# One transformer block on one core: dilated attention reads gathered operands, and the feed-forward part's last features and first tiles change order

## The chip, the cores and the metric

One NeuronCore of a Trainium2 chip runs the whole kernel, one launch. The metric is the device time of that launch in microseconds. Engines are named as in the profile: PE is TensorE (PEld its weight loads), DVE VectorE, ACT ScalarE, POOL GpSimd, SP SyncE, whose queue issues all the DMAs here.

## What is computed

The reference is one layer on x of 2048 tokens by 1024: an RMS norm, one input projection, four mixers side by side (dilated window attention, an RG-LRU, a Mamba-2 SSD, differential attention), an output projection, a norm and a residual, then a feed-forward part with a squared ReLU. Two parts matter here:

```python
DILATED_PATTERNS = ((128, 1), (512, 4), (2048, 16))
...
qb = strided(q)                      # [heads, dil, blocks, 128, 64]: every dil-th token
kc = with_prev(strided(k))           # a block of keys and the one before it
sc = jnp.einsum('bhrnqd,bhrnkd->bhrnqk', qb, kc).astype(jnp.float32) * scale + bias
...
f = jnp.square(jax.nn.relu(jnp.einsum('bsd,df->bsf', u, w_ff_up[layer])))
```

f then goes through w_ff_down, a norm and a residual. All inputs and outputs are f32. The kernel splits f32 operands into f16 high and low parts and adds up to three products of them.

## The kernel before, in words

**Order of work.** No engine's order is written out by hand. The kernel is recorded as many threads in named lanes (Loom, L305); weave (L442) then lists the instructions in the order in which it thinks they can start, and this static order is each engine's program. cost_of (L390) prices an instruction: an f16 matmul by its columns at 2390 a microsecond, whatever its stride; an ACT activation of n elements at 0.065 + n/1195 us; a POOL copy at 0.1 + 2.15 n/1000 us. A lane's priority shifts its planned start by 0.1 us a step (L469); a lower number goes first. All engines, SP included, work off their queues in order, so an instruction that waits holds up what stands behind it.

**Dilated attention** (L1072 to L1233) works on two pairs of heads, g = 0 and 1. dilated_pair loads f16 q, and f16 high and low keys (kh, kl), token by token along the free dimension, in two loads: the first 512 tokens, then the rest. Passes run in the order p = 1, 2, 0, with dil 4, 16 and 1, of 16 blocks each. For a block, dilated_block takes 128 queries as stationary operand, q[hh][:, qv], and 256 keys (128 for a first block) as moving operand, kh[hh][:, kv] and kl[:, hh, kv], where qv and kv are slices with step dil. Per head it adds a high and a low product, so four score matmuls "as" a block. Then DVE adds the bias and takes the extreme, ACT takes the exponential, PE transposes, DVE copies to SBUF, PE multiplies with v ("ao"), and DVE writes the result to its place in num. In pass 1 the blocks with n = 0, which need the first 512 tokens only, come first. After each pass its statistics go through DRAM; pass 0 ends with dilated_merge, whose sums run on POOL. Projections of the other mixers (tiles pt and pv) run in lanes of their own and stand between the blocks on PE.

**Feed-forward part** (class Ffn, L1622 to L1948). It is a seven-product scheme (Strassen's, Winograd's form) on halves of the operands. There are 16 pairs of feature tiles, g = 0 to 15, in PASSES (L37) of 2, 2, 3, 3, 3 and 3 pairs, and two token halves, cp. run (L1919) calls up_weights and up_block for each pair and half, in order of g; the last two blocks are (15, 1) and (15, 0). An up_block has 84 matmuls (lane up, priority 2), puts raw features e into DRAM (put, L1732; not for the pass that is used last), and up_operands (L1773, lane fform, priority 1) forms four sums on POOL (fz), splits seven operands on ACT and DVE (fs) and stores them (fO): for two of the four token tiles j with two stores, or for all four j with four stores in the pass that comes last in QS (L35), pass 5. The down products take the passes in the order QS = 1, 2, 0, 3, 4, 5, and within a pass cp = 0, 1 and j = 0, 1, 2, 3 (L1947). down_weights loads raw rows (dr), takes differences on POOL (ds) and splits them (dw). f_operands (L1814) loads the formed operands of a tile with an even j (fo from fO), and forms those of an odd j from raw features (fr, ft on POOL, then ACT and DVE). down_block (L1835) accumulates in the f32 tiles y. These lie in pool fd:

```python
k.fd = k.pool("fd", after=("fuw", "dk2"))     # L2036: opens when both are done with
```

fuw and dk2 hold the features, the temporaries and the splits of the up part, so y is first written after the last fs. Tiles 1 and up claim their y tiles before their first matmul in the plan.

Of the kernel before, what the change touches and what calls it, by code (L numbers as in the profile page):

```python
# [11 lines left out]
F16 = mybir.dt.float16  # L12
# [7 lines left out]
P = 128  # L20
S = 2048
# [1050 lines left out]
def dilated_attention(k, ap):  # L1072

    nc = k.nc
    bp = k.pool("apm", side="right", on=("w", "u", "stage"), after=("lru",))
    with nc.lane("aload"):
        q = [ap.tile([P, S], F16, tag=f"q{hh}", name=f"aq{hh}") for hh in range(2)]
        kh = [ap.tile([P, S], F16, tag=f"k{hh}", name=f"ak{hh}") for hh in range(2)]
        kl = ap.tile([P, 2, S], F16, tag="kl", name="akl")
    for g in range(2):  # L1080
        dilated_pair(k, ap, bp, g, q, kh, kl)


def token_view(a, dil):
# [5 lines left out]
    return [(slice(r * nb, (r + 1) * nb), v[r]) for r in range(dil)]  # L1090


def dilated_pair(k, ap, bp, g, q, kh, kl):
    nc = k.nc
    ms = ap.tile([P, 2, 2 * NT], F32, tag="ms", name=f"ams{g}")
    ds = ap.tile([P, 2, 2 * NT], F32, tag="ds", name=f"ads{g}")
    num = {}
    with nc.lane("aload"):
        f = score_scale(k, ap, 2 + g)
    for p in (1, 2, 0):  # L1100
        dil = DILS[p]
        nb = NT // dil
        va = k.vA[:, g * P:(g + 1) * P]
        with nc.lane("aload"):
            bias = ap.tile([P, 2, 256], F32, tag="bias", name=f"ab{g}{p}", bufs=2)
            for hh in range(2):
                toeplitz(k, bias[:, hh, :], skewed(k, g * 2 + hh, ND + p * NA, 256), 256, 0, 256)
            nc.gpsimd.tensor_scalar(bias[:], bias[:], f[:, 1:2], 1.0, op0=ALU.mult, op1=ALU.mult)
            v = ap.tile([P, NT, P], F32, tag="v", name=f"av{g}{p}", bufs=2)
            mt = ap.tile([P, NT, 2], F32, tag="mt", name=f"mt{g}{p}", bufs=2)  # L1110
            dt = ap.tile([P, NT, 2], F32, tag="dt", name=f"dt{g}{p}", bufs=2)
            if p:
                nm = num[p] = (ap if p == 1 else bp).tile([P, S], F32, tag=f"num{p}", name=f"num{g}{p}")
            if p == 1:
                for c0, c1 in ((0, 512), (512, S)):
                    sl = slice(c0, c1)
                    for hh in range(2):
                        rows, n = slice(hh * 64, hh * 64 + 64), c1 - c0
                        src = k.qA[g][rows, :, sl]
                        nc.sync.dma_start(q[hh][:, sl], src[0:1, 0:1, 0:1].custom([[S, P], [1, n]], [P, n], src))  # L1120
                        for x, t in ((0, kh[hh][:, sl]), (1, kl[:, hh, sl])):
                            src = k.kA[g][rows, x:x + 1, sl]
                            nc.sync.dma_start(t, src[0:1, 0:1, 0:1].custom([[2 * S, 64], [0, 2], [1, n]], [P, n], src))
                    for ch in range(c0 // 512, c1 // 512):
                        nc.sync.dma_start(v[:, ch:NT:4, :],
                                          va[ch * 512:ch * 512 + 512, :].rearrange("(i r) c -> i r c", r=4))
            elif p == 2:
                nc.sync.dma_start(v[:], va.rearrange("(i r) c -> i r c", r=16))
            else:
                nc.sync.dma_start(v[:], va.rearrange("(n i) c -> i n c", i=P))  # L1130
            if (g, p) == (0, 1):
                k.strips.append(skewed(k, 6, 0, S))
        if p:
            for n in range(nb):
                for r in range(dil):
                    with nc.lane("dil"):
                        dilated_block(k, ap, q, (kh, kl), v, bias, f, mt, dt, nm, 0, dil, r, n, r * nb + n)
            with nc.lane("astat"):
                for src, dst, nme in ((mt, ms, "m"), (dt, ds, "d")):
                    dram = k.dram.tile([S, 2], F32, tag=f"st{nme}{p}", name=f"ast{nme}{g}{p}")  # L1140
                    for sl, a in token_view(dram, dil):
                        nc.sync.dma_start(a, src[:, sl, :])
                    nc.sync.dma_start(dst[:, p - 1, :].rearrange("p (n h) -> p n h", h=2),
                                      dram.rearrange("(n i) h -> i n h", i=P))
            continue
        for ch in range(4):
            with nc.lane("dil"):
                nm = bp.tile([P, 512], F32, tag="num0", name=f"num{g}0{ch}", bufs=2)
                nc.claim(nm)
            for n in range(4 * ch, 4 * ch + 4):  # L1150
                with nc.lane("dil"):
                    dilated_block(k, ap, q, (kh, kl), v, bias, f, mt, dt, nm, ch * 512, 1, 0, n, n)
            with nc.lane("merge"):
                dilated_merge(k, bp, g, ch, nm, num, mt, dt, ms, ds)

# [39 lines left out]
    nc.sync.dma_start(k.mixT[ch][g * P:(g + 1) * P, :], nm[:])  # L1195


def dilated_block(k, ap, q, kt, v, bias, f, mt, dt, num, t0, dil, r, n, b):
    nc = k.nc
    lo = 0 if n else P  # L1200
    qv = slice(n * P * dil + r, n * P * dil + r + (P - 1) * dil + 1, dil)
    k0 = (n * P - (P - lo)) * dil + r
    kv = slice(k0, k0 + (255 - lo) * dil + 1, dil)
    es = []
    ps = k.psum.tile([P, 2, 256], F32, tag="S", name="as", bufs=2)
    with nc.fuse():
        for hh in range(2):
            nc.tensor.matmul(ps[:, hh, lo:256], q[hh][:, qv], kt[0][hh][:, kv], start=True, stop=False)
            nc.tensor.matmul(ps[:, hh, lo:256], q[hh][:, qv], kt[1][:, hh, kv], start=False, stop=True)
    for hh in range(2):  # L1210
        e = ap.tile([P, 256], F32, tag=f"e{hh}", name="ae", bufs=3)
        nc.vector.tensor_tensor_reduce(e[:, lo:256], ps[:, hh, lo:256], bias[:, hh, lo:256], f[:, 0:1], BIG, ALU.add, ALU.min,
                                       mt[:, b, hh:hh + 1])
        nc.scalar.activation(e[:, lo:256], e[:, lo:256], AF.Exp, bias=mt[:, b, hh:hh + 1], scale=-1.0,
                             accum_out=dt[:, b, hh:hh + 1])
        es.append(e)
    tp = turn(k, [P, 2, 256], b, "atp")
    with nc.fuse():
        for hh in range(2):
            for c in range(lo // P, 2):  # L1220
                nc.tensor.transpose(tp[:, hh, c * P:(c + 1) * P], es[hh][:, c * P:(c + 1) * P], k.ident)
    at = ap.tile([P, 2, 256], F32, tag="at", name="aat", bufs=2)
    if ATD(b):
        nc.vector.tensor_copy(at[:, :, lo:256], tp[:, :, lo:256])
    else:
        nc.scalar.activation(at[:, :, lo:256], tp[:, :, lo:256], AF.Copy)
    o = k.psum.tile([P, 512], F32, tag="O", name="ao", bufs=1)
    with nc.fuse():
        for c in range(lo // P, 2):
            for hh in range(2):  # L1230
                nc.tensor.matmul(o[hh * 64:(hh + 1) * 64, 0:P], v[:, b - 1 + c, hh * 64:(hh + 1) * 64],
                                 at[:, hh, c * P:(c + 1) * P], start=(c == lo // P), stop=(c == 1))
    nc.vector.tensor_copy(num[:, qv.start - t0:qv.stop - t0:dil], o[:, 0:P])  # L1233
# [388 lines left out]
class Ffn:  # L1622
# [87 lines left out]
    def up_block(self, g, cp):  # L1710
# [25 lines left out]
                nc.sync.dma_start(self.f[q, cp][j, :, x, :].rearrange("j p c -> p j c"),  # L1736
                                  e[f][:, j].rearrange("p j a t -> p j (a t)"))
        q = next(i for i, (p0, p1) in enumerate(PASSES) if p0 <= g < p1)
        with nc.lane("up", 2):
            X, Y, Z, V = self.banks(False)  # L1740
            nc.need(*u[TURN[-1]])
            s = k.fuw.tile([P, 512], F32, tag="s", name=f"us{g}{cp}", bufs=1)
# [25 lines left out]
            put(0)  # L1768
        self.made_last = e
        if q + cp:  # L1770
            self.up_operands(q, g - PASSES[q][0], cp, e)

    def up_operands(self, q, x, cp, e):  # L1773

        k, nc = self.k, self.k.nc
        with nc.lane("fform", 1, DVE=1.0):
            js = slice(0, 4, 1 if q == QS[-1] else 2)
            nj, ni = (4, 2) if q == QS[-1] else (2, 4)
            if e is None:
# [139 lines left out]
    def run(self):  # L1919
# [2 lines left out]
        self.fst = k.pool("fst", side="right", on=("ub",))  # L1922
        blocks = [(0, 0), (1, 0), (0, 1), (1, 1)] + [(g, cp) for g in range(2, n - 1) for cp in range(2)]
        blocks += [(n - 1, 1), (n - 1, 0)]
        ready = 0
        for g, cp in blocks:
            while ready < min(n, g + 2):
                self.up_weights(ready, 0 if ready < 3 else 1)
                ready += 1
                for x in range(8) if ready == 2 else (ready + 5,) if 2 < ready < 11 else ():  # L1930
                    self.down_top(x)
            self.up_block(g, cp)
            if self.made in (9, 13):
                self.up_operands(0, (self.made - 9) // 4, 0, None)
        self.down_scale()
# [2 lines left out]
        for n, q in enumerate(QS):  # L1938
# [5 lines left out]
                    self.gp = k.wpool.tile([P, D], F32, tag="wraw", name="fgp", bufs=2)  # L1944
                    nc.sync.dma_start(self.gp[:], self.post.to_broadcast([P, D]))
            for cp in range(2):
                for j in range(4):  # L1947
                    self.down_block(q, cp, j)  # L1948


# [131 lines left out]
```

## Time and profile before

| | before |
|---|---|
| median of three runs | 2567.38 us (2563.37 to 2567.38) |
| the profiled execution | 2568.09 us |
| its span, first to last instruction | 2566.3 us |
| mean granted TensorE clock | 0.985 |
| PE, DVE, ACT, POOL busy | 95%, 73%, 50%, 44% of the span |

The profiled execution lies 0.71 us above the median. Almost every instruction carries line 562 (L562), the place where the planner issues, so instructions are told apart by tile names: "as<-ak,aq" is a score matmul that reads the keys' tile ak and the queries' tile aq. Where a row starts with a time, that is the start in us from the span's start, followed by the duration. A matmul's duration includes the pipeline behind it; what one costs PE is the distance between two starts.

### The profile page before, as it was taken

To read this page: it belongs to the slowest core of one execution; us is meant where nothing else is said; L and a number is where in the kernel's file an instruction comes from. 1 tells how busy PE (TensorE), PEld (TensorE's weight loads), DVE (VectorE), ACT (ScalarE), POOL (GpSimd) and SP (SyncE) were. 2 spreads that over 40 slices of the span, in tenths; PEclk is the share of its full clock that TensorE was granted. 3 is DMA by queue.
4 is the path that set the end of the run, shared out by engine and by line. 5 is a ranking of instruction groups with operands and counts; after the bars stand their busy time and mean duration, and the time that the engine had idled before them with its cause. 6 is when DMAs were issued, how large, how long until landed. Compare 5 with 4: busy or idle time off the path is not lost.

```text
span 2566.3 us, 39805 instructions
## 1 busy us (share of the span) xinstructions
PE 2426.2 (95%) x14186; PEld 1285.8 (50%) x14186; DVE 1879.7 (73%) x3985; ACT 1280.9 (50%) x2677; POOL 1120.2 (44%) x1139
## 2 busy tenths in 40 slices
PE   7999999999999998999999999999997999999997
PEld 5555574765744455665445444444443444444443
DVE  6487887776689877867876776666657869868566
ACT  6367765443346667755535555555654413213221
POOL 5274331011155634455541444444435546645356
PEclk9999999999999998999999999999998999999999
DMA  6523215355251345235563444433325423323266
GB/s 190 152 67 93 87 60 166 91 137 125 61 151 60 104 128 150 93 92 164 173 222 108 143 156 142 153 106 109 115 102 184 145 76 109 123 86 124 81 202 194
DMA packets 286262, 322.28 MB, mean 126 GB/s; under 512 B 51508, under 2 KB 237300, under 8 KB 282991
## 3 DMA queue, kind: packets, MB, share of 16 engines
q1 hardware_dynamic: 286063, 319.74, 39.7%
q8 instruction: 112, 1.84, 0.3%
q14 instruction: 87, 0.71, 0.1%
HBM read 219.46 MB, written 107.03 MB: 127 GB/s over the span
## 4 chain that ended last, share of the span: by engine, by line
PE 59%; DVE 18%; DMA 8%; issue 5%; POOL 5%; ACT 3%; SPq 2%; DVEq 0%; POOLq 0%; ACTq 0%
PE mv L562 10%; PE mz L562 10%; PE mx L562 10%; PE my L562 5%; PE pt L562 4%; DVE e L562 4%; PE po L562 2%; DVE y L562 2%; PE as L562 2%; PE pv L562 2%; PE do L562 2%; SPq L562 2%; PE dt L562 2%; PE ao L562 1%; PE atp L562 1%
## 5 line engine op out<-in xcount | busy, mean ns | idle before, releaser
L562 PEld LDWEIGHTS <-fo 128*128 128x128 f16 x2688 | 263.4, 98 | 357.8 <-issue 37.7
L562 PEld LDWEIGHTS <-uw 128*128 128x128 f16 x2688 | 263.7, 98 | 314.4 <-issue 5.2
L562 PE MATMUL pt<-uuh,wl 128*128 128x512 f16 x640 | 243.3, 380 | 1.2 <-DVE wl L562 1.2
L562 PE MATMUL pt<-uuh,wh 128*128 128x512 f16 x640 | 243.6, 381 | 0.5 <-ACT dtraw L562 0.5
L562 PE MATMUL pt<-uul,wh 128*128 128x512 f16 x640 | 243.2, 380 | 0.0
L562 DVE CUSTOM_DVE_ANT_0 e<-sc,strip,scf 128x512 f32<-128x512 f32 (+3 forms) x320 | 205.9, 662 | 24.0 <-PE sc L562 14.4
L562 PE MATMUL mx<-dw,fo 128*128 128x512 f16 x768 | 183.6, 382 | 16.5 <-ACT ds L562 9.8
L562 PE MATMUL mz<-dw,fo 128*128 128x512 f16 x768 | 181.7, 379 | 13.1 <-DVE y L562 13.1
L562 ACT ACTIVATE e<-e,dmn 128x1024 f32<-128x1024 f32 (+4 forms) x192 | 171.4, 894 | 45.3 <-DVE dmn L562 42.6
L562 PEld LDWEIGHTS <-wh 128*128 128x128 f16 x1280 | 122.9, 98 | 126.0 <-issue 21.5
L562 PE MATMUL mv<-dw,fo 128*128 128x512 f16 x768 | 181.4, 379 | 1.9 <-DVE y L562 1.9
L562 POOL TENSOR_TENSOR y<-y,ds 128x512 f32<-128x512 f32 x72 | 112.9, 1584 | 153.7 <-DVE ds L562 153.7
L562 PE MATMUL mx<-u,uw 128*128 128x512 f16 x768 | 177.8, 381 | 2.0 <-DVE c L562 2.0
L562 PE MATMUL mv<-u,uw 128*128 128x512 f16 x768 | 178.3, 381 | 0.0
L562 PE MATMUL mz<-u,uw 128*128 128x512 f16 x768 | 176.5, 379 | 0.2 <-DVE c L562 0.2
L562 PE MATMUL po<-woh,mx 128*128 128x512 f16 x512 | 168.4, 384 | 0.0
L562 POOL TENSOR_SCALAR e<-e,dcf 128x256 f32<-128x256 f32 (+4 forms) x96 | 75.8, 790 | 166.5 <-DVE dcf L562 119.1
L562 ACT ACTIVATE ae<-ae,mt 128x256 f32<-128x256 f32 (+1 forms) x192 | 87.1, 455 | 113.9 <-DVE mt L562 101.8
L562 POOL TENSOR_TENSOR ur<-ur,g_ffn 128x1024 f32<-128x1024 f32 x32 | 62.0, 1942 | 126.9 <-DMA ur<-in_w_ff_up_dram 65.4
L562 PE MATMUL sc<-k,q 128*128 128x512 f16 (+3 forms) x320 | 103.8, 351 | 13.5 <-DVE dmn L562 9.2
L562 PEld LDWEIGHTS <-mx 128*128 128x128 f16 x768 | 76.0, 100 | 78.2 <-issue 4.8
L562 ACT ACTIVATE at<-dt 128x512 f32<-128x512 f32 (+3 forms) x160 | 80.9, 528 | 68.5 <-PE dt L562 64.3
(338 smaller groups left out, 5646.8 us busy)
## 6 DMA issues: line engine op xcount, KB each, us to landing
dr<-in_w_ff_down_dram SPq DMA_DIRECT2D x64, 512.0 KB, 3.6
fo<-fO SPq DMA_DIRECT2D x20, 1344.0 KB, 5.6
fO<-fs SPq DMA_DIRECT2D x44, 512.0 KB, 3.0
ur<-in_w_ff_up_dram SPq DMA_DIRECT2D x32, 512.0 KB, 6.0
wr<-in_w_in_dram SPq DMA_DIRECT2D x24, 512.0 KB
fD<-e SPq DMA_DIRECT2D x48, 256.0 KB, 2.3
fO<-fs SPq DMA_DIRECT2D x26, 384.0 KB, 2.8
fr<-fD SPq DMA_DIRECT2D x12, 768.0 KB, 4.2
```

Of the source, the lines that this page charges most:

```text
L562: op.ins.append(fn(*[real(a) for a in args], **{n: real(a) for n, a in kw.items()}))
```

## The change

In the dilated attention q, kh and kl become one tile each with both heads. For passes 1 and 2, the 16 blocks go in four chunks of four: in pass 1 a chunk is one residue r of the tokens and its four blocks n; in pass 2 it is four residues. For each chunk, gathered copies 128x2x512 elements of q on ACT, and of kh and kl on POOL, into tiles in which the chunk's tokens are neighbours (three buffers each). The score matmuls then read neighbours. Where blocks go in num, the statistics and v is as before. Pass 0 reads the loaded tiles as before.

In the feed-forward part, the pairs of features are made in the order 0 to 9, 13, 14, 15, 10, 11, 12; the last two up blocks, and their up_operands, get priority -1; and in the first down pass tiles j go 0, 2, 1, 3.

```diff
-        q = [ap.tile([P, S], F16, tag=f"q{hh}", name=f"aq{hh}") for hh in range(2)]
-        kh = [ap.tile([P, S], F16, tag=f"k{hh}", name=f"ak{hh}") for hh in range(2)]
-        kl = ap.tile([P, 2, S], F16, tag="kl", name="akl")
+        ops = [ap.tile([P, 2, S], F16, tag=t, name=f"a{t}") for t in ("q", "kh", "kl")]
...
+def gathered(k, ap, ops, dil, c, name):
+    nc = k.nc
+    out = []
+    for t, a in zip(("q", "kh", "kl"), ops):
+        d = ap.tile([P, 2, 512], F16, tag=f"{t}g", name=f"a{t}g{name}{c}", bufs=3)
+        n = 4 * dil // 16
+        if n == 1:
+            o, i = d[:], a[:, :, c:S:dil]
+        else:
+            o = d[:].rearrange("p h (r i) -> p h r i", r=n)
+            i = a[:].rearrange("p h (i r) -> p h r i", r=dil)[:, :, n * c:n * c + n, :]
+        if t == "q":
+            nc.scalar.activation(o, i, AF.Copy)
+        else:
+            nc.gpsimd.tensor_copy(o, i)
+        out.append(d)
+    return out
...
-            for n in range(nb):
-                for r in range(dil):
+            for c in range(4):
+                with nc.lane("aperm"):
+                    part = gathered(k, ap, ops, dil, c, f"{g}{p}")
+                for i in range(4):
+                    r, n = (c, i) if p == 1 else (4 * c + i, 0)
                     with nc.lane("dil"):
-                        dilated_block(k, ap, q, (kh, kl), v, bias, f, mt, dt, nm, 0, dil, r, n, r * nb + n)
+                        dilated_block(k, ap, part, i * P, v, bias, f, mt, dt, nm, 0, dil, r, n, r * nb + n)
...
-    k0 = (n * P - (P - lo)) * dil + r
-    kv = slice(k0, k0 + (255 - lo) * dil + 1, dil)
+    qs, ks = slice(at0, at0 + P), slice(at0 - P + lo, at0 + P)
...
-            nc.tensor.matmul(ps[:, hh, lo:256], q[hh][:, qv], kt[0][hh][:, kv], start=True, stop=False)
-            nc.tensor.matmul(ps[:, hh, lo:256], q[hh][:, qv], kt[1][:, hh, kv], start=False, stop=True)
+            nc.tensor.matmul(ps[:, hh, lo:256], q[:, hh, qs], kh[:, hh, ks], start=True, stop=False)
+            nc.tensor.matmul(ps[:, hh, lo:256], q[:, hh, qs], kl[:, hh, ks], start=False, stop=True)
...
-        with nc.lane("up", 2):
+        last = self.made >= 2 * self.pairs - 2
+        with nc.lane("up", -1 if last else 2):
...
-            self.up_operands(q, g - PASSES[q][0], cp, e)
+            self.up_operands(q, g - PASSES[q][0], cp, e, -1 if last else 1)
-    def up_operands(self, q, x, cp, e):
+    def up_operands(self, q, x, cp, e, prio=1):
...
-        with nc.lane("fform", 1, DVE=1.0):
+        with nc.lane("fform", prio, DVE=1.0):
...
+        turn = [*range(10), 13, 14, 15, 10, 11, 12]
...
-                self.up_weights(ready, 0 if ready < 3 else 1)
+                self.up_weights(turn[ready], 0 if ready < 3 else 1)
...
-            self.up_block(g, cp)
+            self.up_block(turn[g], cp)
...
-                for j in range(4):
+                for j in (0, 2, 1, 3) if n == 0 else range(4):
                     self.down_block(q, cp, j)
```

## Rows read from the trace of the kernel before

**Rows 1.** The page: its span and the busy time of PE.

```profile
span 2566.3 us, 39805 instructions
...
PE 2426.2 (95%) x14186; PEld 1285.8 (50%) x14186; DVE 1879.7 (73%) x3985; ACT 1280.9 (50%) x2677; POOL 1120.2 (44%) x1139
```

**Rows 2.** Busy time by stage: us, each engine (instructions), granted clock, DMA share, GB/s.

```profile
430.00:715.00 285.00, 276.06 (x2336) 181.55 (x2335) 199.62 (x733) 123.36 (x428) 37.54 (x31) 0.98 0.45 114
715.00:1000.00 285.00, 269.92 (x1694) 148.99 (x1693) 231.77 (x628) 180.45 (x399) 147.99 (x192) 0.99 0.36 109
...
1915.00:2003.00 88.00, 68.80 (x299) 29.65 (x298) 67.48 (x95) 47.99 (x91) 42.63 (x36) 0.92 0.46 156
...
1951.00:1961.00 10.00, 0.33 (x2) 0.05 (x1) 2.43 (x5) 3.15 (x8) 6.87 (x6) 0.64 0.08 28
```

**Rows 3.** Timeline of PE, pass 1, a projection, pass 2, pass 0: start, us.

```profile
446.17 0.41 PE L562 MATMUL as<-ak,aq 128*128 128x256 f16 x1
446.40 0.41 PE L562 MATMUL as<-akl,aq 128*128 128x256 f16 x1
...
473.52 0.22 PE L562 MATMUL pv<-wh,uul 128*128 128x128 f16 x1
...
473.63 0.22 PE L562 MATMUL pv<-wl,uuh 128*128 128x128 f16 x1
...
503.47 0.42 PE L562 MATMUL as<-akl,aq 128*128 128x128 f16 x1
503.71 0.42 PE L562 MATMUL as<-ak,aq 128*128 128x128 f16 x1
...
527.37 0.27 PE L562 MATMUL as<-akl,aq 128*128 128x256 f16 x1
527.48 0.27 PE L562 MATMUL as<-ak,aq 128*128 128x256 f16 x1
```

**Rows 4.** Waits of PE, 1915 to 2003 us: in total, times, longest.

```profile
PE mx L562 <- ACT ds L562: 9.8, 1, 9.8
PE mx L562 <- DMA fo<-fO: 3.8, 2, 3.5
PE mx L562 <- DVE fo L562: 2.4, 1, 2.4
PE my L562 <- DVE dw L562: 2.1, 1, 2.1
```

**Rows 5.** Timeline of PE at the turn to the down products.

```profile
1915.48 2.75 PE L562 MATMUL mx<-u,uw 128*128 128x512 f16 x12
...
1961.11 2.72 PE L562 MATMUL mx<-dw,fo 128*128 128x512 f16 x6 [9.78 <-ACT ds L562]
```

**Rows 6.** Instructions on tile as: ns min/median/max, first and last start.

```profile
L562 PE MATMUL as<-ak,aq x192: 218/394/443, 431.2 to 714.0; 128*128 128x256 f16 x108, 128*128 128x128 f16 x84
```

**Rows 7.** Groups by form: busy us, mean ns, idle before.

```profile
L562 POOL TENSOR_SCALAR e<-e,dcf 128x256 f32<-128x256 f32 x40 | 40.7, 1017 | 116.9 <-DVE dcf L562 76.6 <-DVE dmn L562 21.8 <-DVE s_wi L562 6.0
...
L562 POOL TENSOR_SCALAR xt<-xt,rs_x 128x1024 f32<-128x1024 f32 x16 | 19.0, 1190 | 1.6
...
L562 ACT ACTIVATE mx<-o 128x1024 f16<-128x1024 f32 x16 | 16.9, 1056 | 0.6
```

**Rows 8.** The chain that ended last: start us, us, what.

```profile
569.06 8.81 DMA akl<-kA
...
1924.33 6.97 DMA dr<-in_w_ff_down_dram
```

**Rows 9.** Timeline of ACT at the turn to the down products.

```profile
1957.91 2.19 ACT L562 ACTIVATE fs<-fz 128x512 f16<-128x512 f32 x4 [6.85 <-POOL fz L562]
1960.00 0.58 ACT L562 ACTIVATE y<-mx 128x512 f32<-128x512 f32 x1
```

**Rows 10.** Timeline of SP's DMA issues at the turn.

```profile
1948.56 12.90 SPq L562 DMA_DIRECT2D fO<-fs  x4
...
1966.63 0.32 SPq L562 DMA_DIRECT2D fo<-fO  x1
```

**Rows 11.** Waits of POOL, 430 to 715 us: in total, times, longest.

```profile
POOL num L562 <- DVE cb L562: 47.9, 4, 20.2
```

More of the change, by code (lines that the diff above doesn't have):

```diff
@@ L1076, in dilated_attention @@
     with nc.lane("aload"):
-        q = [ap.tile([P, S], F16, tag=f"q{hh}", name=f"aq{hh}") for hh in range(2)]
-        kh = [ap.tile([P, S], F16, tag=f"k{hh}", name=f"ak{hh}") for hh in range(2)]
-        kl = ap.tile([P, 2, S], F16, tag="kl", name="akl")
+        ops = [ap.tile([P, 2, S], F16, tag=t, name=f"a{t}") for t in ("q", "kh", "kl")]
     for g in range(2):
-        dilated_pair(k, ap, bp, g, q, kh, kl)
+        dilated_pair(k, ap, bp, g, ops)
 def token_view(a, dil):
@@ L1090, in token_view, with dilated_pair @@
     return [(slice(r * nb, (r + 1) * nb), v[r]) for r in range(dil)]
-def dilated_pair(k, ap, bp, g, q, kh, kl):
+def gathered(k, ap, ops, dil, c, name):
     nc = k.nc
+    out = []
[13 more added lines that the diff above has]
+    return out
+def dilated_pair(k, ap, bp, g, ops):
+    nc = k.nc
+    q, kh, kl = ops
     ms = ap.tile([P, 2, 2 * NT], F32, tag="ms", name=f"ams{g}")
@@ L1119, in dilated_pair @@
                         src = k.qA[g][rows, :, sl]
-                        nc.sync.dma_start(q[hh][:, sl], src[0:1, 0:1, 0:1].custom([[S, P], [1, n]], [P, n], src))
-                        for x, t in ((0, kh[hh][:, sl]), (1, kl[:, hh, sl])):
+                        nc.sync.dma_start(q[:, hh, sl], src[0:1, 0:1, 0:1].custom([[S, P], [1, n]], [P, n], src))
+                        for x, t in ((0, kh[:, hh, sl]), (1, kl[:, hh, sl])):
                             src = k.kA[g][rows, x:x + 1, sl]
@@ L1151, in dilated_pair @@
                 with nc.lane("dil"):
-                    dilated_block(k, ap, q, (kh, kl), v, bias, f, mt, dt, nm, ch * 512, 1, 0, n, n)
+                    dilated_block(k, ap, ops, n * P, v, bias, f, mt, dt, nm, ch * 512, 1, 0, n, n)
             with nc.lane("merge"):
@@ L1195, in dilated_merge, with dilated_block @@
     nc.sync.dma_start(k.mixT[ch][g * P:(g + 1) * P, :], nm[:])
-def dilated_block(k, ap, q, kt, v, bias, f, mt, dt, num, t0, dil, r, n, b):
+def dilated_block(k, ap, ops, at0, v, bias, f, mt, dt, num, t0, dil, r, n, b):
     nc = k.nc
+    q, kh, kl = ops
     lo = 0 if n else P
     qv = slice(n * P * dil + r, n * P * dil + r + (P - 1) * dil + 1, dil)
-    k0 = (n * P - (P - lo)) * dil + r
-    kv = slice(k0, k0 + (255 - lo) * dil + 1, dil)
+    qs, ks = slice(at0, at0 + P), slice(at0 - P + lo, at0 + P)
     es = []
```

## The prediction

> **What bounds the kernel now.** I read the page first. TensorE (PE) is busy for 95% of the span [rows 1], so time goes only where PE's own work shrinks or where it stands still. Next I read busy time by stage. In the dilated stage, 430 to 715 us, PE is busy 276 of 285 us, VectorE (DVE) 200, ScalarE (ACT) 123 and GpSimd (POOL) 38 [rows 2]: PE is the bound, and POOL is nearly free. Around the turn from the up to the down products, 1915 to 2003 us, PE is busy only 69 of 88 us at a mean clock of 0.92 [rows 2]. These are the two places that the change touches.
>
> In the first place the timeline of PE shows what a score matmul costs when its operands lie apart. Back to back, from start to start, it is 0.23 us for 256 columns of every 4th token, 0.24 us for 128 columns of every 16th, 0.11 us for 256 neighbouring tokens, and 0.055 us for 128 neighbouring columns (two projection matmuls, the same form) [rows 3]. PE spends the difference reading, not multiplying. In the second place PE's waits are the reading: four causes make 18.1 us [rows 4], and after the longest, 9.8 us, six matmuls take 2.72 us [rows 5], where six of 512 columns need about 1.3 (twice 0.11 us each, by [rows 3]). [...] That is another 1.4 us, so 19.5 us in all.
>
> **The change part by part.** *Score matmuls.* There are 192 high and 192 low ones [rows 6], 64 of each per pass over both head pairs. Of pass 1 (every 4th token) 96 are 256 wide and 32 are 128 wide; all 128 of pass 2 are 128 wide; pass 0 is not changed. Reading gathered neighbours, they should cost what pass 0 and the projections show: 96 x (0.23 - 0.11) = 11.5 us; 32 x 0.06 (half of that saving, as half the columns) = 1.9 us; 128 x (0.24 - 0.055) = 23.7 us. Together 37 us of PE time. The planner prices an f16 matmul by columns alone (cost_of, L390), so the order that it wrote already assumed the cheap ones; nothing has to be reordered for the gain.
>
> [...] Every 4th f16 value is 8 bytes from the next, and it costs 0.23 against 0.11 us [rows 3]. [...]
>
> *The copies.* Sixteen chunks, each one copy on ACT and two on POOL, all 128x1024. ACT's nearest row is 1056 ns for 128x1024 f16 [rows 7]: 17 us, which an engine busy 123 of 285 us hides; were that cover gone, it would be 17 us at most. No row shows POOL copying f16 with a stride. The one-input row of the same size gives 1.19 us; the worst per element is 128x256 in 1017 ns, so 4.1 us [rows 7]. I take 2 us, nearer the row of the same size: 64 us on an engine with 247 idle. Three buffers let copies run chunks ahead. The 96 blocks take 285 us, 3 us each, so a chunk of four lasts 12 us and needs 2 POOL copies of 2 us: hidden, but for the first chunk of a pass.
>
> *The start of a pass.* Before, the first four blocks of pass 1 need only the first 512 tokens. Now the first chunk takes every 4th of all 2048, so it waits for the second load (8.8 us from issue to landing [rows 8]) and then for two POOL copies. Queued behind a waiting copy stand POOL's bias scaling, weight scaling and merge sums; behind the first scores, DVE and ACT's whole block. Projection matmuls stand between the blocks on PE and fill the gap. Bounds for each head pair: 0, or 8.8 + 4 = 13 us with no filler. I take 3, since PE idles little in this stage, so 6 us. Pass 2 finds its tokens loaded.
>
> *Other engines.* With 37 us less, DVE's 200 us fill 81% of the stage. The next stage, 715 to 1000, has that same share, and there PE idles 5.3% against 3.1% here [rows 2]; 2.2% of 248 us is 5 us lost. The dilated part nets 37 - 6 - 5 = **26 us**, between 0 (all waits, below) and 37.
>
> *The turn to the down products.* The last up block starts on PE at 1915.48 [rows 5]; its 84 matmuls need 84 x 0.22 = 18.5 us, but first down matmuls are put between them, which wait 3.8 us for fo and 2.1 us for dw [rows 4]. Its features therefore finish late, ACT splits the last forms at 1957.9, and only then does it write y [rows 9], since pool fd opens after fuw and dk2 are done (L2036). With priority -1 the block ends at about 1934. The last features are now those of pass 4: their forms are half as wide (two of four j), with two stores instead of four on SP's queue, and two stores of raw features are added. Activations (2 us), POOL (four ops, some 3 us) and the splits (3 us) give y at about 1942. PE meanwhile has one product of the first down tile and then needs weights whose rows land at 1931.3 [rows 8] and still pass POOL, ACT and DVE: some 3 us idle. The second tile is now j = 2, which only loads, so the 2.4 us wait for DVE's fo goes; but its load stands on SP behind the stores of the last forms, as the earlier one stood 12.9 us behind four of them [rows 10]; I leave 3.5 us for that. 19.5 - 6.5 = **13 us**, between -4 (the loads behind stores cost more than now) and 19.5. That pass 5's wider forms (four stores each) come three pairs earlier costs nothing: the same work, in an up stage where PE never waits on them.
>
> *Moving tiles 1 and 3 together* makes two formed operands follow each other, each formed beside one tile's products; bounded by the present 2.4 us wait either way, taken as 0.
>
> **Sum.** The profiled execution took 2568.1 us (span 2566.3, the rest around it), 0.7 above the median of 2567.4. 2568.1 - 26 - 13 = **2529 us**.
>
> **The rivals.** *A block's own chain takes over.* Score, DVE, ACT, transpose, DVE, product: if it sets the pace, PE merely waits where it was slow. For it: DVE at 81% and one-buffer results. Against: PE idles only 9 of 285 us now. Then the stage gives 10 us: 2568.1 - 10 - 13 = 2545.
>
> *The turn's idle only moves*, because down's loads now stand behind more of the up block's stores on SP. For: the 12.9 us on SP [rows 10]. Against: the wait on ACT has a plain cause that goes. 2568.1 - 26 = 2542.
>
> *POOL becomes the pace, and the kernel slower.* After the change a chunk lasts (285 - 37) / 24 = 10.3 us. If the strided copies take c, 16 chunks stretch by 16 x (2c - 10.3); at c = 6.6 us this is 46 us and eats the 39 us and the 0.2% bound, and at 7 us it gives 2529 + 59 = 2588. For: POOL's queue is in order, and a merge sum stood at its head for 20.2 us waiting for DVE [rows 11]. Against: the worst row gives 4.1 us [rows 7]. [...]
>
> *Nothing to measure:* both gains fail together, or a reshuffled order loses as much elsewhere: about 2565.
>
> **Chances.** Forecast 0.56 (own range 2511 to 2548: dilated 15 to 37, turn 5 to 19.5), chain 0.15, moved idle 0.18, nothing 0.05, POOL 0.06. The range is 2508 to 2556: it leaves out the last two and a little at each end. A measurement here tells 0.2% (5 us) from no change; faster by more is 0.56 + 0.15 + 0.18 = 0.89, within 0.05, slower 0.06.
>
> **What would show it.** Right: score matmuls 0.11 us (256) and 0.055 us (128) apart in all passes; some 32 POOL copies near 2 us and 16 ACT copies near 1.1 us; the last block starting near 690 instead of 714; PE's waits after 1900 (now shifted by 26) under 8 us, and no ACT wait of 9.8. Wrong: POOL copies over 4 us, PE waiting for the gathered tiles, or PE standing on fo behind SP's stores.

## The result and the profile after

The change takes 2525.46 us (median of six runs, 2524.67 to 2531.34) against 2567.38: a ratio of 0.9835, 95% interval 0.9816 to 0.9854. In what follows a kernel's gain or loss is its ratio to the kernel before, measured beside it, times 2568 us; the change is then worth -42.4 us, give or take 5. The profiled execution took 2525.43 us.

Two lines of the page and the same stretches as in [rows 1, 2], for the change:

```profile
span 2523.6 us, 39843 instructions
...
PE 2387.6 (95%) x14186; PEld 1271.8 (50%) x14186; DVE 1882.1 (75%) x3985; ACT 1293.9 (51%) x2691; POOL 1186.3 (47%) x1171
```

Busy time by stage (the last stretch is that of 1915 to 2003 before, shifted by 34 us):

```profile
430.00:715.00 285.00, 269.59 (x2520) 180.38 (x2519) 223.50 (x779) 155.36 (x463) 108.52 (x82) 1.00 0.50 126
715.00:1000.00 285.00, 253.00 (x1578) 147.05 (x1577) 230.80 (x606) 179.17 (x382) 144.41 (x186) 0.95 0.42 122
1881.00:1969.00 88.00, 79.51 (x350) 34.82 (x349) 73.12 (x107) 47.07 (x94) 43.77 (x38) 0.96 0.50 171
```

PE does 38.6 us less work (2426.2 to 2387.6), with as many matmuls. POOL, ACT and DVE are busier in the first stretch, where more now happens, and at the turn PE is busy 79.5 of 88 us instead of 68.8.

The timeline of PE in pass 1 shows what answers to [rows 3], 128 columns and 256 columns (start, duration):

```profile
460.19 0.22 PE L562 MATMUL as<-aklg,aqg 128*128 128x128 f16 x1
460.24 0.22 PE L562 MATMUL as<-akhg,aqg 128*128 128x128 f16 x1
...
460.46 0.27 PE L562 MATMUL as<-aklg,aqg 128*128 128x256 f16 x1
460.57 0.27 PE L562 MATMUL as<-akhg,aqg 128*128 128x256 f16 x1
```

They start 0.055 and 0.11 us apart, as neighbours did before. The views of the three gathered tiles give the copies (ns min/median/max):

```profile
L562 POOL COPY akhg<-akh x16: 1095/1979/2102, 441.5 to 613.7; 128x1024 f16<-128x1024 f16 x16
...
L562 POOL COPY aklg<-akl x16: 1107/2071/2125, 442.5 to 615.7; 128x1024 f16<-128x1024 f16 x16
...
L562 ACT ACTIVATE aqg<-aq x16: 1117/1612/2125, 440.0 to 613.6; 128x1024 f16<-128x1024 f16 x16
```

A copy of every 16th token takes about 2.1 us on either engine. One of every 4th takes 1.1 us on ACT, and on POOL in twelve of sixteen; the other four, all near the start of the first pass 1, take 1.6 to 2.1 us, as this one:

```profile
442.50 2.12 POOL L562 COPY aklg<-akl 128x1024 f16<-128x1024 f16 x1
```

What slows these four is not shown. PE waits for a gathered tile once, 0.6 us.

At the turn, PE's waits, 1881 to 1969 us (in total, times, longest):

```profile
PE mz L562 <- DVE y L562: 4.7, 3, 3.6
PE my L562 <- ACT dw L562: 3.1, 1, 3.1
PE my L562 <- DVE dw L562: 0.6, 1, 0.6
```

and the timeline of PE:

```profile
1881.79 2.75 PE L562 MATMUL mx<-u,uw 128*128 128x512 f16 x12
...
1897.33 2.75 PE L562 MATMUL mv<-u,uw 128*128 128x512 f16 x12
1899.92 1.46 PE L562 MATMUL mx<-dw,fo 128*128 128x512 f16 x6
...
1905.13 0.38 PE L562 MATMUL my<-dw,fo 128*128 128x512 f16 x1 [3.11 <-ACT dw L562]
...
1916.51 1.97 PE L562 MATMUL mz<-dw,fo 128*128 128x512 f16 x6 [3.55 <-DVE y L562]
```

and that of ACT, which answers to [rows 9]:

```profile
1911.81 1.33 ACT L562 ACTIVATE fs<-fz 128x256 f16<-128x256 f32 x4 [2.58 <-POOL fz L562]
...
1913.66 0.57 ACT L562 ACTIVATE y<-mx 128x512 f32<-128x512 f32 x1
```

In the same stretch before, the waits make 18.1 us by the four causes of [rows 4], 19.3 with three small ones; these are all of them now, 8.4 us. And y is written 31.9 us after the last up block starts (1881.79 to 1913.66), against 44.5 before [rows 5, 9]. The last block starts 33.7 us earlier than before, the span ends 42.7 us earlier: by this one pair of executions some 34 us come from ahead of the turn and 9 from the turn.

### The profile page after: what moved, and what is told of

Read it like the earlier page. It is cut to its first block, busy times and chain, and to the rows that moved or that the text cites. A ratio compares the mean times of both kernels' runs of the same rounds, so it can differ in the third digit from the quotient of the medians.

```text
span 2523.6 us, 39843 instructions
## 1 busy us (share of the span) xinstructions
PE 2387.6 (95%) x14186; PEld 1271.8 (50%) x14186; DVE 1882.1 (75%) x3985; ACT 1293.9 (51%) x2691; POOL 1186.3 (47%) x1171
## 4 chain that ended last, share of the span: by engine, by line
PE 38%; DVE 10%; issue 3%; POOL 2%; ACT 2%; DMA 2%; SPq 0%; DVEq 0%; POOLq 0%; ACTq 0%
PE mz L562 9%; PE mv L562 9%; PE mx L562 9%; PE my L562 5%; DVE y L562 3%; PE po L562 3%; DVE fs L562 1%; DVE dw L562 1%; POOL fz L562 1%; PE fut L562 1%; DVE fo L562 1%; DMA fr<-fD 1%; POOL ds L562 0%; DVE c L562 0%; ACT e L562 0%
## 5 line engine op out<-in xcount | busy, mean ns | idle before, releaser
L562 POOL TENSOR_TENSOR ur<-ur,g_ffn 128x1024 f32<-128x1024 f32 x32 | 64.0, 2003 | 121.5 <-DMA ur<-in_w_ff_up_dram 54.3
L562 POOL TENSOR_TENSOR fz<-e,e 128x256 f32<-128x256 f32 (+1 forms) x30 | 27.5, 917 | 198.5 <-ACT e L562 154.6
L562 ACT ACTIVATE ae<-ae,mt 128x128 f32<-128x128 f32 (+1 forms) x192 | 86.7, 455 | 63.5 <-DVE mt L562 56.1
L562 ACT ACTIVATE e<-c 128x512 f32<-128x512 f32 x96 | 60.1, 626 | 112.6 <-DVE c L562 112.5
```

The source lines that it names most:

```text
L562: op.ins.append(fn(*[real(a) for a in args], **{n: real(a) for n, a in kw.items()}))
```

## The experiments

Every experiment but the last, steps_2_8, was timed in five rounds against the kernel before. In the table, "us" is the ratio's distance from 1 times 2568.

| kernel | median, us | ratio (95%) | us |
|---|---|---|---|
| the change | 2525.5 | 0.9835 (0.9816 to 0.9854) | -42 |
| gather_only | 2537.8 | 0.9878 (0.9862 to 0.9895) | -31 |
| ffn_only | 2556.5 | 0.9956 (0.9941 to 0.9972) | -11 |
| near_reads | 2536.3 | 0.9875 (0.9858 to 0.9893) | -32 |
| copies_twice | 2597.0 | 1.0108 (1.0090 to 1.0125) | +28 |
| twice_half | 2546.2 | 0.9912 (0.9896 to 0.9929) | -23 |
| once_double | 2584.2 | 1.0062 (1.0050 to 1.0075) | +16 |
| no_prio | 2527.3 | 0.9832 (0.9817 to 0.9847) | -43 |
| no_turn | 2539.3 | 0.9883 (0.9871 to 0.9896) | -30 |
| no_js | 2524.6 | 0.9837 (0.9814 to 0.9860) | -42 |
| pass2_only | 2528.1 | 0.9849 (0.9826 to 0.9872) | -39 |
| price_measured | 2529.8 | 0.9853 (0.9828 to 0.9879) | -38 |

**The two halves apart.** gather_only is the change with the feed-forward part as before (priorities 2 and 1, features 0 to 15, tiles 0 to 3 in order):

```diff
-        with nc.lane("up", -1 if last else 2):
+        with nc.lane("up", 2):
...
-        turn = [*range(10), 13, 14, 15, 10, 11, 12]
+        turn = [*range(16)]
...
-                for j in (0, 2, 1, 3) if n == 0 else range(4):
+                for j in range(4):
```

> The change's dilated part alone: gathered copies and neighbouring reads, the feed-forward part in its old order. Theory (PE's strided reading was the cost, the copies are hidden, the turn gave 9 us): the last up block starts 33.7 us earlier with the whole change, so this one should take 2567.4 - 33.7 = about 2534 us (2530 to 2539), with score matmuls 0.11 and 0.055 us apart. Rival (much of the 42 us is the feed-forward order, or a lucky re-planning): above 2545 us.

ffn_only is the reverse: the kernel before with just these lines of the change.

> The feed-forward part of the change alone (priority of the last two up blocks and their forms, order of the features, order of the first down tiles), dilated attention as before. Theory: 42.5 - 33.7 = 9 us faster, 2558 us (2553 to 2563), with PE's wait of 9.8 us on ACT gone. Rival (the turn's idle only moves, and the 42 us are all the gathering): 2565 to 2569 us.

Measured: -31 and -11 us, together the change's -42. The halves add up.

**What the copies and the later start cost.** near_reads is the kernel before (no copies, old order of blocks) whose passes 1 and 2 read neighbouring tokens in place, so that their scores are those of other tokens:

```diff
-    k0 = (n * P - (P - lo)) * dil + r
-    kv = slice(k0, k0 + (255 - lo) * dil + 1, dil)
+    a0 = (n * dil + r) * P
+    qs, ks = slice(a0, a0 + P), slice(a0 - P + lo, a0 + P)
...
```

> The kernel before, but passes 1 and 2 read neighbouring tokens of the loaded tiles in place of every 4th or 16th one, without any copy and in the old order of blocks: the scores of these two passes are of other tokens than the reference's. It gives the reading cost by itself. Theory: 37 us of PE time go and most of it shows: 2528 to 2536 us, 0 to 6 us better than the gathered dilated part alone, the difference being the price of copies and of the later start of a pass. Rival (a block's own chain through DVE and ACT takes over the pace): no better than 2545 us, with PE waiting on DVE in the dilated stage.

Measured: -32 us. With the copies and the wait for the second load it is -31. The two intervals overlap almost wholly, so both together cost less than the runs can tell: 1 us, give or take 6.

**Twice the copies.** copies_twice makes every copy twice, into the same tile:

```diff
             nc.scalar.activation(o, i, AF.Copy)
+            nc.scalar.activation(o, i, AF.Copy)
         else:
             nc.gpsimd.tensor_copy(o, i)
+            nc.gpsimd.tensor_copy(o, i)
```

> The whole change with every gathering copy done twice into the same tile (16 more on ACT, 32 more on POOL, some 25 and 55 us of busy time). Theory (hidden work): 2525 to 2530 us, only the first chunk of a pass comes 2 to 4 us later. Rival (POOL is close to being the pace, as a chunk of four blocks lasts 10 us and its four POOL copies would last 4.4 to 8.4 us beside POOL's other work): 2540 us or more.

Measured: 70 us slower than the change (+28 against -42). That much can't be work on POOL alone: 32 more copies there take 53 us (32 at 1.67 us), and PE's waits did not name them. But the planner also saw twice the price and wrote another order. The next two runs keep the one and alter the other.

**Work or price.** twice_half copies twice, each at half its price in the plan; once_double copies once, at twice its price:

```diff
+            for _ in range(2):
+                nc.gpsimd.tensor_copy(o, i)
+                nc.ops[-1].cost /= 2
...
             nc.gpsimd.tensor_copy(o, i)
+            nc.ops[-1].cost *= 2
```

The first edit is twice_half's, the second once_double's; the copies on ACT are edited alike.

> Every gathering copy done twice, as in copies_twice (2597 us), but the planner is told half the price for each, so that the order of all instructions is close to that of the whole change and only the real work is doubled. Theory P (the 71 us of copies_twice came from the plan: priced at 2.3 us each, POOL became the pace of the dilated lanes in the planned order, and the order of the queues kept it): 2525 to 2535 us. Theory W (POOL and ACT really run out of time): 2575 us or more.

> The opposite: one copy each, as in the whole change, but priced at twice in the plan, so that the order is close to that of copies_twice without its work. Theory P: 2575 to 2597 us, with the dilated blocks ending far behind 690 us. Theory W: 2525 to 2532 us.

Measured against the change: 20 us slower with the doubled work, between what the two theories gave, and 58 us slower with the doubled price and not one copy or matmul more. Most of the 70 us is the order. The 20 us need not all be work, since this order, too, is only close to the change's. The windows of once_double show where, first once_double's two stretches, then the change's in the next fence:

```profile
430.00:690.00 260.00, 246.28 (x2195) 159.01 (x2194) 181.37 (x566) 130.19 (x348) 97.73 (x78) 0.99 0.49 127
...
860.00:1110.00 250.00, 193.61 (x1291) 140.93 (x1292) 170.75 (x487) 156.33 (x318) 101.93 (x136) 0.82 0.30 85
```

```profile
430.00:690.00 260.00, 244.59 (x2370) 167.70 (x2369) 205.07 (x729) 145.56 (x442) 98.35 (x70) 1.00 0.51 128
...
860.00:1110.00 250.00, 225.74 (x1578) 148.51 (x1576) 191.27 (x515) 160.51 (x332) 113.20 (x142) 0.94 0.40 116
```

To 690 us PE is as busy in both, but with other work: as the plan has it, a chunk comes late, and projections (pt) stand there. Their last matmul starts at 863 us instead of 947, the last score matmul at 787 instead of 690. From 860 us on there is nothing left to lay between the links of the mixers' chains: PE is busy 194 of 250 us, and the granted clock falls to a mean of 0.82. So a price moved 58 us, by using the filler up too early.

**Prices as measured.** price_measured tells the plan what the trace says of a copy:

```diff
+        nc.ops[-1].cost = 1.1 if dil == 4 else 2.05
```

> The change with its copies priced in the plan as the trace has them, on ACT and on POOL: 1.1 us in pass 1 and 2.05 us in pass 2 (the plan has 0.92 for ACT and 2.3 for POOL in both). Nothing that runs is altered but the order. If the plan's price is what made the doubled price cost 59 us, and the effect goes on below today's price, a price on POOL that is lower by 1.2 us for 16 copies (and 0.25 for the other 16; 23 us in all, where doubling added 74) gives up to 10 us: 2515 to 2524. Rival: the price matters only where the planned copies fill POOL's queue, and the reshuffled order is as good as another: 2525 within 5 us.

Measured: 2529.8 us, 5 us above the change with overlapping intervals, so no gain. Its last score matmul starts at 677 us, 13 us earlier than in the change, but its first output product at 1009.7 instead of 1002.9, so the time is given back between. The rival holds, as far as one lower price can show it: below today's price the order is as good as another.

**Pass 2 alone.** pass2_only lets pass 1 read every 4th token in place, in the old order of blocks:

```diff
...
-                    r, n = (c, i) if p == 1 else (4 * c + i, 0)
+                    r, n = (i, c) if p == 1 else (4 * c + i, 0)
-                        dilated_block(k, ap, part, i * P, v, bias, f, mt, dt, nm, 0, dil, r, n, r * nb + n)
+                        dilated_block(k, ap, ops if p == 1 else part, None if p == 1 else i * P, v, bias, f, mt, dt, nm, 0,
+                                      dil, r, n, r * nb + n)
...
```

> The change with the copies and neighbouring reads in pass 2 alone; pass 1 reads every 4th token in place, its blocks in the old order (those with n = 0 first). By the distances of matmuls pass 1's part of the gain is 11.5 + 1.9 = 13.4 us; less 3 us a head pair for the later start it would be 7 us. Theory A (the start of a pass and the copies cost almost nothing, as the run without copies suggested): about 13 us slower than the change, 2538 (2534 to 2541), score matmuls end some 13 us later. Theory B (the prediction's 6 us for the start of pass 1): 7 us slower, 2532 (2529 to 2535). Rival C: pass 1's saving is hidden by what the blocks wait for on other engines: within 3 us of the change, 2525.

Measured: 2528.1 us, 3 to 4 us above the change (the intervals overlap). That is nearest to rival C: pass 1's 13.4 us of matmul time are worth about a quarter of that, though by the two intervals it may be anything up to some 11 us. The windows from the first score matmul to the first output product (po), both ends taken 0.24 us ahead, show where PE stands still, first pass2_only, then the change, then the kernel before:

```profile
427.30:999.53 572.23, 534.76 (x4103) 330.12 (x4102) 451.15 (x1395) 330.43 (x839) 233.25 (x255) 0.98 0.46 124
```

```profile
443.60:1002.64 559.04, 512.68 (x4049) 322.74 (x4047) 446.59 (x1375) 327.81 (x838) 250.95 (x266) 0.97 0.45 119
```

```profile
430.93:1037.79 606.86, 571.04 (x4189) 348.71 (x4189) 465.55 (x1437) 329.55 (x868) 207.09 (x248) 0.97 0.42 116
```

PE stands still 37.5 us in the first (572.23 - 534.76) and 46.4 in the second: gathering in pass 1, too, came with 9 us more idle time. In the kernel before it is 35.8 us. In near_reads, where the score matmuls are as cheap as in the change, the same stretch has only 38.2 (574.44 - 536.23). So the cheaper matmuls alone do not make PE stand still. What else gathering in pass 1 changes does: its copies, the later start or the order of blocks; which of them is not shown. Nor is this idle time simply lost, since the windows hold different amounts of work (4049 matmuls in the change's, 4189 before), and near_reads is no faster than gather_only.

**The parts of the turn.** no_prio gives the last up blocks and their operands the old priorities:

```diff
-        with nc.lane("up", -1 if last else 2):
+        with nc.lane("up", 2):
-            self.up_operands(q, g - PASSES[q][0], cp, e, -1 if last else 1)
+            self.up_operands(q, g - PASSES[q][0], cp, e, 1)
```

> The whole change without the priority of the last two up blocks and their forms (back to 2 and 1). Theory (the priority is what keeps down's matmuls out of the last up block, so y is written early): loses most of the turn's 11 us, 2532 to 2538 us, with a long wait of PE on ACT back. Rival (the lighter last forms of pass 4 do it): 2525 to 2529 us.

no_turn makes the features in the old order, and keeps the priority and the order of tiles:

```diff
-        turn = [*range(10), 13, 14, 15, 10, 11, 12]
+        turn = [*range(16)]
```

> The whole change with the features in the order 0 to 15, so that the last forms are pass 5's wide ones with four stores each. Theory (the priority is the main part): loses 2 to 5 us, 2527 to 2531 us, the last forms' POOL and store work being longer ahead of the first y. Rival (the order of features is the main part): 2533 us or more.

no_js has the tiles of the first down pass in the old order:

```diff
-                for j in (0, 2, 1, 3) if n == 0 else range(4):
+                for j in range(4):
```

> The change with the tiles of the first down pass in their old order 0, 1, 2, 3. The prediction gave the new order a gain: the wait of 2.4 us for DVE's formed operand goes, and 0 is lost for moving tiles 1 and 3 together. By that: 2 to 3 us slower than the change, about 2528, and the wait of PE for DVE's fo (2 us or more) is back near 1915 to 1960. Rival: the order of features alone did it, and tile 1 is formed in time now that the last forms are lighter: 2525 within 3 us, no wait for DVE's fo over 1 us. Second rival: the new order puts the loads behind stores and costs something: 2 us or more faster than the change.

Measured: without the priority -43 us and with the old tiles -42, both as the change (and no wait for DVE's fo came back with the old tiles); without the order of features -30, which is gather_only's -31. So the order of features is the whole gain of the turn that can be measured; no run has it alone. PE's four longest waits in no_turn, 1860 to 1990 us:

```profile
PE my L562 <- ACT dw L562: 9.8, 1, 9.8
PE my L562 <- DVE dw L562: 4.0, 1, 4.0
PE mz L562 <- DVE y L562: 2.5, 2, 1.7
PE mx L562 <- DVE dw L562: 1.9, 1, 1.9
```

The 9.8 us are back, for another cause. Here the last up block is not interrupted either (its last matmuls start at 1902.34), and the first down product waits all the same, now for weights, since their splits (dw) stand on ACT behind those of the last forms (fs from fz). ACT's timeline in no_turn:

```profile
1916.08 2.19 ACT L562 ACTIVATE fs<-fz 128x512 f16<-128x512 f32 x4 [4.49 <-POOL fz L562]
1918.17 2.14 ACT L562 ACTIVATE dw<-ds,kd 128x512 f16<-128x512 f32 x3
...
1930.21 0.60 ACT L562 ACTIVATE y<-mx 128x512 f32<-128x512 f32 x1 [6.88 <-PE mx L562]
```

In the change the last forms' splits are half as wide and done at 1913, and the weights' stand ahead of them (1904.36 to 1908.75). In no_prio the block is cut up as before, and that costs little, because what lies between its pieces is down products that have to be done anyway. PE's waits there:

```profile
PE mx L562 <- ACT ds L562: 5.6, 1, 5.6
PE mx L562 <- DMA fo<-fO: 1.7, 1, 1.7
PE mz L562 <- DVE y L562: 1.7, 2, 1.4
PE mx L562 <- DVE fo L562: 0.2, 1, 0.2
```

That is 9.2 us, near the change's 8.4. y is written 43.4 us after the start of the last up block in no_turn (1886.80 to 1930.21), 36.3 in no_prio (1887.24 to 1923.55), 31.9 in the change and 44.5 before.

**What a stride costs.** steps_2_8 is the kernel before with other strides, so that passes 1 and 2 score other tokens. It was timed once (2559.98 us); what counts here is its trace:

```diff
...
+    step = {1: 1, 4: 2, 16: 8}[dil]
+    w = (256 - lo) * step
+    a0 = {1: n * P, 4: n * 512 + r * 2 + 1, 16: r}[dil]
+    k0 = {1: n * P - P + lo, 4: max(0, n * 512 - 1), 16: r}[dil]
+    qs, ks = slice(a0, a0 + (P - 1) * step + 1, step), slice(k0, k0 + w - step + 1, step)
...
```

> The kernel before with score matmuls of other tokens: pass 1 reads every 2nd token instead of every 4th, pass 2 every 8th instead of every 16th, so the scores of passes 1 and 2 are those of other queries and keys; number and size of matmuls are as before. What a moving operand costs by its stride: if a line of 16 bytes costs 1.9 ns however many of its values are used (every 4th: 2 a line, 0.23 us for 256; every 16th: 1 a line, 0.24 us for 128), then every 2nd, 4 a line, costs 0.12 us for 256, and every 8th, 1 a line, 0.24 us for 128, as every 16th. Rival: the cost grows with the stride itself: about 0.16 to 0.17 us for 256 at every 2nd, and about 0.14 us for 128 at every 8th (between 0.115 at every 4th and 0.24 at every 16th).

The timeline of PE, 256 columns of every 2nd token, then 128 of every 8th:

```profile
455.10 0.28 PE L562 MATMUL as<-ak,aq 128*128 128x256 f16 x1
455.22 0.28 PE L562 MATMUL as<-akl,aq 128*128 128x256 f16 x1
...
500.20 0.41 PE L562 MATMUL as<-ak,aq 128*128 128x128 f16 x1
500.44 0.41 PE L562 MATMUL as<-akl,aq 128*128 128x128 f16 x1
```

From start to start it is 0.117 us (116 to 118 ns within a block) and 0.23 us, as the theory had it for 64 and 128 pieces of 16 bytes (0.12 and 0.24). The rival gave 0.16 and 0.14.

No version here beats the change. The change without its priorities, or with its tiles in the old order, is as fast and simpler.

## Why the prediction was right

Forecast 2529 us, measured 2525.5, by the case that it held likeliest. Its two terms came out at 31 for 26 (gather_only) and 11 for 13 (ffn_only); that these errors go opposite ways, and that the total lies within 4 us, is luck in part. Point by point:

- **Score matmuls, 37 us of PE time.** Right: the distances are 0.11 and 0.055 us, and PE's busy time fell by 38.6. That the sum fits so closely is chance: in near_reads, with the same distances, it fell by 32.4 (to 2393.8).
- **Copies.** POOL's 2 us holds for pass 2, and most copies of pass 1 cost 1.1; ACT's 1.06 holds for pass 1 alone, pass 2 costs 2.1. In all POOL takes 54.5 us (32 at 1733 and 1677 ns) for the 64 forecast and ACT 25.5 for 17. That they are hidden is right as far as near_reads can tell. The cover is thinner than a chunk's 12 us against 2 copies of 2 us said: copies made twice cost 20 us, with 2.2 to 4.2 us of POOL in the place of each copy, where the rival's sum loses nothing up to 5.15 (half of 10.3) and the whole gain at 6.6.
- **The start of a pass, 6 us.** Probably too much: copies and start together cost 1 us, give or take 6. The first score matmul did start 13 us later (443.8 against 431.2), as the upper bound had it, and projections filled the gap.
- **Other engines, 5 us.** Not confirmed: the cause named did not show. In time the dilated part lost 6 of its 37 us, give or take 4 (it gave 31), where the forecast took off 11 in all. PE's idle time between the first score and the first output product did grow, by 10.6 us (35.8 to 46.4). But the forecast put that down to DVE's share once PE is faster, and in near_reads, where PE is as fast, it grew by 2.4 (to 38.2). Most of the loss seems to be pass 1's: its 13.4 us brought 3 to 4, where the steps gave 7. Why pass 2 alone brings some 28 us (-39, less the turn's 11), more than its 23.7 us of matmuls, stays open; both ends are within the intervals.
- **The turn, 13 us.** The sum was near (11), the step was not. The forecast named the priority first (the block done at about 1934, y at 1942, 26.5 us after the block's start; it is 31.9). The block did end as said, 18.1 us after its start (1881.79 to 1899.92; 18.5 forecast), but y came 13.7 us behind that instead of 8: on ACT a split of weights (dw) waits 1.65 us for POOL ahead of the last activation (done at 1905.59), and the four forms on POOL take 4.6 us (1907.21 to 1911.78) for some 3. The runs show that the priority is worth nothing measurable and that without the order of features, which makes the last forms lighter, the gain is gone. Of the 3.8 us that the forecast read as waits for fo inside the block, 0.3 lies behind it (at 1973). The 3.5 us for a load behind stores did not come: SP's stores of the last forms take 2.98 us and PE waits for no load. In their place PE waits 3.55 us for DVE's y. The weights' 3 us came (3.1 and 0.6). The order of tiles, forecast to remove 2.4 us, removed nothing that can be told.
- **The signs named ahead.** The last score block starts at 690, as said. The waits at the turn are 8.4 us where under 8 was said, and no ACT wait of 9.8 is left.
- **The rivals.** A block's own chain as the pace would have left 10 us of the dilated part; it gave 31. The moved idle would have left nothing at the turn; it gave 11. POOL as the pace did not come, but a mere planner's price of 4.6 us (twice 2.3) would have made the kernel slower than before by 16 us: once_double. The forecast had a reshuffled order only as what might cancel the gain, at 0.05, and said that nothing has to be reordered; that an order written by a wrong price can lose more than the gain was among none of the rivals.

## What to carry to other kernels

Where a matmul's moving operand lies as far apart as here, gather it first on an engine with room: the 48 copies of 1.1 to 2.1 us ran beside PE's work, where near_reads could not tell them from nothing (1 us, give or take 6), while PE paid for the stride in every product (0.23 us for 0.11 at every 4th token, 0.24 for 0.055 at every 16th). In a kernel whose order is planned, check a new instruction's price as closely as its work, since the price alone moved 58 us. At a change of stage, look at how heavy the last piece of work is before changing who goes first.

## What the runs showed of the hardware

What a strided moving operand (the keys) cost PE, from start to start, goes with the pieces of 16 bytes that it touches: in steps_2_8 256 columns of every 2nd f16 token took 117 ns for 64 pieces and 128 of every 8th 233 for 128, and in the kernel before 256 of every 4th took 230 for 128 and 128 of every 16th 240 for 128. That is 1.80 to 1.88 ns a piece; with pieces of 8 bytes it would be 0.90 to 1.88, with 32 bytes 1.88 to 3.66, so of the three only 16 bytes fit these four strides. Neighbours took 109 ns for 256 columns and 55 for 128. The queries, the stationary operand, were strided too, but in pass 1 before, with the same queries, 128 columns of keys are 0.12 us apart, where 256 are 0.23 [rows 3]:

```profile
432.73 0.30 PE L562 MATMUL as<-ak,aq 128*128 128x128 f16 x1
432.85 0.30 PE L562 MATMUL as<-akl,aq 128*128 128x128 f16 x1
```

On ACT and POOL a stride showed later. A copy of every 4th value took 1.1 us for 1024 values in most cases, where the nearest rows of neighbours take 1.06 and 1.19 [rows 7], and one of every 16th about twice as much (2.06 to 2.13 us, about 2 ns a value). On PE 256 columns of every 4th token already took 230 ns, where neighbours took 109.

The granted clock was lower where the order left PE without filler: a mean of 0.82 from 860 to 1110 us in once_double, with PE busy 194 of 250 us, and 0.94 in the change, with 226. Matmuls behind a standstill were slower. In once_double the same two (mcbp) take 0.79 us at 896.05 and 0.39 at 907.03. In the kernel before, six (mx<-dw,fo) take 2.72 us behind the wait of 9.78 [rows 5], with the clock at 0.50 from 1961.0 to 1963.6 us, and ahead of it six of the same size (mv<-dw,fo) take 1.46 at 1949.87, with the clock at 1.00 from 1948 to 1951. In these two cases PE's standstill was paid twice, in idle time and in slower matmuls behind it.
